# Norm sums in the accumulators of the second layer, and weights loaded in half tiles

## The chip, the core and the metric

The kernel is one program on one core of a Trainium2 chip. The metric is the device time of one execution in microseconds (us), the median of several runs. One further execution was recorded by the hardware profiler; durations of single instructions come from it.

The engines are named as in the profile: PE is TensorE, which multiplies matrices and writes to PSUM; DVE is VectorE, ACT is ScalarE, POOL is GpSimd, and SP is SyncE, which issues all DMAs of this kernel. Each engine works through its own queue strictly in order: an instruction that waits holds up all that stand behind it.

## What is computed

The reference is a trunk of two layers over a sequence of 1024 tokens with 1024 channels, in float32. A layer is a mixer and a feed-forward net (FFN), each wrapped in a norm ahead of it and a norm behind it, whose result is added to the residual:

```
for l in range(2):
    y = rms_norm(h, norm_g[l, 0])
    y = even_mixer(y, ...) if l == 0 else odd_mixer(y, ...)   # y @ w_in, two head groups, cat @ w_out
    h = h + rms_norm(y, norm_g[l, 1])
    y = swiglu(rms_norm(h, norm_g[l, 2]), w_gate[l], w_up[l], w_down[l])
    h = h + rms_norm(y, norm_g[l, 3])
```

`rms_norm(x, g)` is `x * rsqrt(mean(x*x) + 1e-6) * g`, the mean over the 1024 channels of one token. The even mixer has a gated DeltaNet group and a sparse attention group that an indexer selects keys for; the odd mixer has a stick-breaking attention group and a gated linear recurrence (HGRN2).

## The kernel before

**Tiles.** Everything is held feature-major: a tile is 128 channels by 512 tokens, so the residual of one half of the sequence (512 tokens) is 8 tiles. The two halves go through the layers one behind the other and overlap. A weight unit is 128x1024 numbers (512 KB). `wload` (L228) brings it in as one tile `wraw` and splits each number into a high part `whi` (ACT, L193) and a rest `wlo` (DVE for the first 512 columns, POOL for the others, L197). Activations are split in the same way (`yhi`, `ylo`, or two `act` tiles). `passes` (L240) then multiplies high with high, high with rest and rest with high into one bank of PSUM; a unit that makes one tile of 128x512 takes 24 matmuls of 128x512.

**Banks.** PSUM has 8 banks of 128x512. `banks` (L137) shares them out by name, and the kernel does it once: three accumulators (`acc`), one bank `a` for the recurrences, one bank `b`, three banks `w` for the attention. A name with several banks hands them out in turn: the fourth `acc` gets the bank of the first, and its first matmul waits until that one has been read.

**Norms.** The sum over the 1024 channels is a matmul with a tile of ones. The squares of the 8 tiles are made on ACT and added up on DVE into the tile `ssq` (`sumsq`, L290). `inv_rms` (L302) multiplies `ssq` with the ones into a bank, and ACT makes the reciprocal root of it (tile `rs` or `rd`). In the residual and in `norms` (L346) that bank is `b`, which the first stage also uses for DeltaNet chunks.

**Residual.** `residual` (L376) stands behind each output projection and each FFN. It takes a first sum (over the sublayer's output, L380), scales the 8 tiles on DVE (L388), adds the 8 tiles of the residual, which come by DMA into 3 buffers `hld` (L387, L389), and takes a second sum over the result, for the next norm. In the form with `late=True` (behind an FFN of the first layer) all of it is one piece: scaling, adding, the next activation tiles (`y_tile`, L332 on ACT and L336 on DVE), the squares and the second sum (`norms`, L351), and the same sum as a column (L317).

**Order.** A scheduler decides the order on each engine: it simulates the program and takes, among the instructions that are ready in its simulation, those with the highest priority. Code under `first()` has a raised priority. The order is fixed when the kernel is built. The code that matters for the second stage is in `run` (L1279): after `m0.close()` (L1316) the recurrence and stick-breaking attention of the second layer follow, mixed with the rest of the first layer for the second half: `outproj(0, 1)`, `after_out(0, 1)`, `proj_c(0)`, four `stick`s, `ffn(0)`, `after_ffn(0, 1)` with `late=True`, `outproj(1, 0)`, and so on. Output projections (`outproj`, L410) work on two accumulators at a time; the second half of an FFN is eight accumulations, of 12 matmuls each in groups of four units.

**The start.** `first_norm(0)` (L360) loads the first half of x in 8 tiles, makes activation tiles without waiting for the norm, and takes the sums alongside. `proj_even_a` (L566) then computes the unit `U_KI` and twelve units `U_QKV` from them.

Of the kernel before, what the change touches and what calls it, by code (L numbers as in the profile page):

```python
# [13 lines left out]
F32R = mybir.dt.float32r  # L14
# [8 lines left out]
P = 128  # L23
# [4 lines left out]
KD = 8  # L28
# [83 lines left out]
class Trunk:  # L112
# [37 lines left out]
    def consts(self):  # L150
# [6 lines left out]
        with self.first():  # L157
            nc.sync.dma_start(self.gg, self.ins["p_cols"])
            nc.sync.dma_start(self.cc, self.ins["c_main"])
        self.k = self.t(self.np_, [P, 8], "kk")  # L160
# [67 lines left out]
    def wload(self, u):  # L228
        nc = self.nc
        with self.first():  # L230
            raw = self.t(self.wp, [P, 1024], "wraw")
            nc.sync.dma_start(raw, self.ins["w_units"][u])
            w = []
            for c, e in ((slice(0, 512), nc.vector), (slice(512, 1024), nc.gpsimd)):
                w.append(self.split(raw[:, c], *(self.t(self.wp, [P, 512], n, F32R, bufs=4) for n in ("whi", "wlo")), (e,)))
        self.pace()

        return lambda o, n=P: [t[:, o % 512:o % 512 + n] for t in w[o // 512]]

    def passes(self, sums, w, first=True, last=True):  # L240

        mm = self.nc.tensor.matmul
        order = [((0, 0), (0, 1)), ((1, 0),)] if w == 0 else [((0, 0), (1, 0)), ((0, 1),)]
        n = len(sums[0][2]) // 2
        seq = [(g, ps, l[a], r[b]) for pairs in order for part in (slice(0, n), slice(n, None))
               for a, b in pairs for g, ps, terms in sums for l, r in terms[part]]
        begun, end = set(), {g: i for i, (g, *_) in enumerate(seq)}
        for i, (g, ps, l, r) in enumerate(seq):  # L250
            mm(ps, l, r, start=first and g not in begun, stop=last and end[g] == i)  # L251
            begun.add(g)
# [11 lines left out]
    def dense_fm(self, u, y):  # L264
        w = self.wload(u)
        ps = self.acc()
        self.passes([(0, ps, [(w(k * P), y.t[k]) for k in range(KD)])], 0)
        return ps

    def dense_tm(self, u0, y):  # L270
# [75 lines left out]
    def norms(self, y, tiles, rows):  # L346

        acc = None
        for k in range(KD):
            acc = self.sumsq(acc, k, tiles[k])  # L350
        y.r = self.inv_rms(acc, "rd", "b")  # L351
        if rows:
            y.rows = self.inv_rms_rows(acc, "b")

# [5 lines left out]
    def first_norm(self, half):  # L360
        with self.first():
            tiles, acc, y = [], None, Y()
            for k in range(KD):
# [4 lines left out]
                else:  # L368
                    acc = self.sumsq(acc, k, x)
                tiles.append(x)  # L370
            if half:
                return self.to_y(0, 0, tiles, self.inv_rms(acc))
# [3 lines left out]
    def residual(self, l, i, src, dst, parts, acc, nxt, box, late=False):  # L376

        nc = self.nc
        with self.first():
            r = self.inv_rms(acc, "rs", "b")  # L380
            acc = None
# [16 lines left out]
        if nxt is not None and not late:  # L398
            yield
            with self.first():  # L400
                r = self.inv_rms(acc, "rs", "b")
            yield
# [101 lines left out]
    def last_residual(self, src, dst, parts, halves):  # L504
        nc = self.nc
        with self.first():
# [4 lines left out]
            for i, (c, acc) in enumerate(halves):  # L511
                r = self.inv_rms(acc, ("rs", "rd")[i], "b")
                for k in range(KD):
# [52 lines left out]
    def proj_even_a(self, half, y):  # L566
        nc = self.nc
        if half == 0:
# [3 lines left out]
            self.an = self.head_gain(self.cp, "a_norm")  # L572
        ps = self.dense_fm(U_KI, y)
        with self.first():
# [11 lines left out]
        for ct in range(12):  # L586
            ps = self.dense_fm(U_QKV + ct, y)
            with self.first():
# [690 lines left out]
    def run(self):  # L1279
        tc = self.tc  # L1280
        every = lambda gen: deque(gen, maxlen=0)
        self.dn = self.head_gain(self.cp, "d_norm")
        self.banks(acc=3, a=1, b=1, w=3)
        m0 = ExitStack()
        pool = m0.enter_context(tc.tile_pool(name="m0", bufs=1))
# [29 lines left out]
        self.finish()  # L1315
        m0.close()  # L1316
        m1 = ExitStack()
        pool = m1.enter_context(tc.tile_pool(name="m1", bufs=1))
# [145 lines left out]
```

## Time and profile before

| What | us |
|---|---|
| median of 3 runs | 2910.11 (2907.5 to 2910.74) |
| the profiled execution, its own time | 2903.69 |
| its span, first to last instruction | 2901.9 |
| PE busy | 2818.6 (97%) |
| DVE busy | 1694.5 (58%) |
| ACT busy | 1574.0 (54%) |
| POOL busy | 1123.3 (39%) |

The span is what the trace covers; 1.8 us of the execution's own time lie around it. The profiled execution was 6.4 us (0.2%) shorter than the median of the runs. Busy time of PE is a sum over matmuls that overlap each other in a pipeline, so what tells of a loss is time in which PE is not busy, and the clock that it was granted.

### The profile page before, as it was taken

The page shows a single profiled execution, that of the slowest core. Times are in us where ns is not written, and L with a number is a line of the kernel's source. Part 1 is how long each engine was busy: PE and PEld are TensorE (multiplying, and loading weights), DVE is VectorE, ACT ScalarE, POOL GpSimd, SP SyncE. Part 2 cuts the span into 40 slices and gives each one's busy share as a digit, 9 for nine tenths or more (in the row PEclk, how much of TensorE's full clock was granted, in tenths as well). Part 3 has the DMA queues.
Part 4 walks back from the last instruction along what each step waited for, and adds up shares of the span by engine and source line. Part 5 has one row for each costly group of instructions (what it writes and reads, how often), then busy time and mean ns, then how long its engine had stood idle before and what let it go on. Part 6 is the DMA issues. An engine that isn't in the chain of part 4 may idle for free. (4 is left out here: it accounts for less than half of the span.)

```text
span 2901.9 us, 41648 instructions
## 1 busy us (share of the span) xinstructions
PE 2818.6 (97%) x14850; PEld 2351.2 (81%) x14850; DVE 1694.5 (58%) x3037; ACT 1574.0 (54%) x2893; POOL 1123.3 (39%) x916
## 2 busy tenths in 40 slices
PE   8999999999999998999999999999999999999997
PEld 6888888878787886978788888889778778788886
DVE  7857973675656557378665235736666544732235
ACT  5545863666657585254664335536666544543333
POOL 3323332344435342255554332325555432333332
PEclk9999999999999999999999999999999999999999
DMA  5433446243333334446333334654323323543233
GB/s 196 136 121 109 144 151 209 91 146 114 103 117 107 104 121 137 139 147 202 111 109 95 100 97 125 231 156 128 98 87 107 98 89 115 167 149 98 95 95 109
DMA packets 200975, 366.63 MB, mean 126 GB/s; under 512 B 16544, under 2 KB 104640, under 8 KB 200768
## 3 DMA queue, kind: packets, MB, share of 16 engines
q1 hardware_dynamic: 200768, 363.97, 39.6%
q8 instruction: 117, 1.92, 0.3%
q14 instruction: 90, 0.74, 0.1%
HBM read 306.23 MB, written 57.67 MB: 125 GB/s over the span
## 5 line engine op out<-in xcount | busy, mean ns | idle before, releaser
L197 POOL TENSOR_TENSOR wlo<-wraw,whi 128x512 fp32r<-128x512 f32 x422 | 589.1, 1396 | 1240.3 <-PE acc L251 497.3
L193 ACT ACTIVATE whi<-wraw 128x512 fp32r<-128x512 f32 x844 | 521.6, 625 | 487.0 <-PE acc L251 431.2
L197 DVE TENSOR_TENSOR wlo<-wraw,whi 128x512 fp32r<-128x512 f32 x422 | 337.9, 801 | 470.7 <-PE acc L251 355.5
L251 PE MATMUL acc<-yhi,whi 128*128 128x512 f32 x2064 | 585.3, 400 | 11.8 <-ACT whi L193 8.0
L251 PE MATMUL acc<-ylo,whi 128*128 128x512 f32 x2064 | 581.9, 398 | 2.2 <-DVE ylo L336 2.2
L251 PE MATMUL acc<-yhi,wlo 128*128 128x512 f32 x2064 | 536.1, 396 | 0.0
L251 PE MATMUL acc<-act,whi 128*128 128x512 f32 (+1 forms) x1984 | 510.6, 393 | 21.3 <-DVE stage L452 5.7
L251 PEld LDWEIGHTS acc<-yhi,whi 128*128 128x128 f32 x2064 | 386.1, 189 | 99.5 <-ACT whi L193 8.0
L251 PEld LDWEIGHTS acc<-ylo,whi 128*128 128x128 f32 x2064 | 386.3, 189 | 88.3 <-issue 6.0
L251 PEld LDWEIGHTS acc<-yhi,wlo 128*128 128x128 f32 x2064 | 383.7, 188 | 84.1 <-issue 6.1
L251 PEld LDWEIGHTS acc<-act,whi 128*128 128x128 f32 x1984 | 363.1, 189 | 109.3 <-issue 11.5
L251 PE MATMUL acc<-act,wlo 128*128 128x512 f32 (+1 forms) x992 | 266.6, 386 | 1.4 <-POOL wlo L197 1.4
L251 PEld LDWEIGHTS acc<-act,wlo 128*128 128x128 f32 x992 | 182.0, 188 | 38.5 <-POOL wlo L197 1.8
L950 ACT ACTIVATE pen<-sc,tk 128x384 bf16<-128x384 f32 (+4 forms) x155 | 155.3, 1002 | 52.2 <-DVE tk L954 46.1
L480 DVE TENSOR_TENSOR part<-acc,part 128x512 f32<-128x512 f32 x152 | 103.8, 685 | 66.2 <-PE acc L251 66.0
L193 ACT ACTIVATE act<-stage 128x512 fp32r<-128x512 f32 x104 | 65.2, 629 | 136.9 <-DVE stage L459 117.0
L197 POOL TENSOR_TENSOR act<-stage,act 128x512 fp32r<-128x512 f32 x88 | 120.2, 1366 | 43.1 <-ACT act L193 41.0
L299 DVE TENSOR_TENSOR ssq<-ssq,sq 128x512 f32<-128x512 f32 (+1 forms) x119 | 98.7, 830 | 27.2 <-ACT sq L298 25.0
L951 DVE TENSOR_SCALAR tk<-tk 128x1 uint32<-128x1 f32 x186 | 39.3, 211 | 125.4 <-ACT pen L950 124.9
L452 DVE TENSOR_TENSOR stage<-acc,stage 128x512 f32<-128x512 f32 x66 | 45.5, 689 | 98.3 <-ACT stage L220 98.2
L251 PE MATMUL acc<-whi,yhi 128*128 128x256 f32 x640 | 100.1, 287 | 1.6 <-DVE stage L552 1.6
L251 PE MATMUL acc<-whi,ylo 128*128 128x256 f32 x640 | 101.3, 287 | 0.0
(461 smaller groups left out, 4038.1 us busy)
## 6 DMA issues: line engine op xcount, KB each, us to landing
wraw<-in_w_units_dram SPq DMA_DIRECT2D x422, 512.0 KB, 3.6
h<-part SPq DMA_DIRECT2D x40, 256.0 KB, 3.9
hld<-h SPq DMA_DIRECT2D x40, 256.0 KB, 4.6
qkvT<-stage SPq DMA_DIRECT2D x24, 256.0 KB, 2.5
kT<-kbT SPq DMA_DIRECT2D x24, 256.0 KB, 3.6
vv<-vb SPq DMA_DIRECT2D x24, 256.0 KB, 3.0
qkv<-qkvT SPq DMA_DIRECT2D x18, 256.0 KB, 3.6
part<-in_x_dram SPq DMA_DIRECT2D x16, 256.0 KB, 6.3
```

The costliest lines, as they stand in the source:

```text
L193: nc.scalar.activation(hi, src, AF.Copy)
L197: e.tensor_tensor(out=lo[:, c], in0=src[:, c], in1=hi[:, c].bitcast(F32), op=OP.subtract)
L251: mm(ps, l, r, start=first and g not in begun, stop=last and end[g] == i)
L299: nc.vector.tensor_tensor(out=acc, in0=acc, in1=sq, op=OP.add)
L452: nc.vector.tensor_tensor(out=s, in0=pg, in1=s, op=OP.mult)
L480: nc.vector.tensor_tensor(out=parts[d], in0=ps, in1=parts[d], op=OP.add)
L950: sc.activation(pen, s, AF.Sign, scale=sg, bias=nb, accum_out=n)
L951: v.tensor_scalar(rej.bitcast(U32), n, th, float(1 << b), op0=OP.is_lt, op1=OP.mult)
```

## The change

Five edits. (1) After the first stage the banks are shared out anew: four `acc`, one `a`, three `w` and no `b`; a new field `nb` names the bank of the norms' sums, `b` in the first stage and `acc` in the second. (2) A weight unit comes in two half tiles of 128x512 (256 KB), four buffers in place of two of double the size. (3) The first two units, `U_KI` and the first `U_QKV`, are loaded together and multiplied side by side, one channel tile after the other (`dense_pair`). (4) The DMA of the constants `c_main` is issued behind the tiles of x. (5) In `passes` the last third of a product (high times rest of the weight) is no longer cut in two halves when several sums are open.

```diff
@@ consts
             nc.sync.dma_start(self.gg, self.ins["p_cols"])
-            nc.sync.dma_start(self.cc, self.ins["c_main"])
@@ wload
-            raw = self.t(self.wp, [P, 1024], "wraw")
-            nc.sync.dma_start(raw, self.ins["w_units"][u])
             w = []
             for c, e in ((slice(0, 512), nc.vector), (slice(512, 1024), nc.gpsimd)):
-                w.append(self.split(raw[:, c], *(self.t(self.wp, [P, 512], n, F32R, bufs=4) for n in ("whi", "wlo")), (e,)))
+                raw = self.t(self.wp, [P, 512], "wraw", bufs=4)
+                nc.sync.dma_start(raw, self.ins["w_units"][u][:, c])
+                w.append(self.split(raw, *(self.t(self.wp, [P, 512], n, F32R, bufs=4) for n in ("whi", "wlo")), (e,)))
@@ passes
-    def passes(self, sums, w, first=True, last=True):
+    def passes(self, sums, w, first=True, last=True, steps=2):
...
-        n = len(sums[0][2]) // 2
-        seq = [(g, ps, l[a], r[b]) for pairs in order for part in (slice(0, n), slice(n, None))
-               for a, b in pairs for g, ps, terms in sums for l, r in terms[part]]
+        n = len(sums[0][2]) // steps
+        parts = [slice(i * n, (i + 1) * n) for i in range(steps)]
+        high, low = order
+        seq = [(g, ps, l[a], r[b]) for part in parts for a, b in high for g, ps, terms in sums for l, r in terms[part]]
+        seq += [(g, ps, l[a], r[b]) for a, b in low for g, ps, terms in sums for l, r in terms]
@@ new
+    def dense_pair(self, us, y):
+        ws, pss = [self.wload(u) for u in us], [self.acc() for _ in us]
+        self.passes([(i, ps, [(w(k * P), y.t[k]) for k in range(KD)]) for i, (w, ps) in enumerate(zip(ws, pss))], 0, steps=KD)
+        return pss
@@ norms, residual, last_residual
-        y.r = self.inv_rms(acc, "rd", "b")
+        y.r = self.inv_rms(acc, "rd", self.nb)
...
-            r = self.inv_rms(acc, "rs", "b")
+            r = self.inv_rms(acc, "rs", self.nb)
@@ first_norm
+            if half == 0:
+                self.nc.sync.dma_start(self.cc, self.ins["c_main"])
@@ proj_even_a
-        ps = self.dense_fm(U_KI, y)
+        ps, first = self.dense_pair((U_KI, U_QKV), y) if half == 0 else (self.dense_fm(U_KI, y), None)
...
-            ps = self.dense_fm(U_QKV + ct, y)
+            ps = first if half + ct == 0 else self.dense_fm(U_QKV + ct, y)
@@ run
         self.banks(acc=3, a=1, b=1, w=3)
+        self.nb = "b"
...
         m0.close()
+        self.banks(acc=4, a=1, w=3)
+        self.nb = "acc"
```

**PE's queue between the FFN of the first layer (second half) and the output projection behind it.** The names: `acc_...<-act_...,whi_...` or `wlo_...` is a matmul of the FFN or of the projection, `b_...<-ssq_...` or `acc_...<-ssq_...` a norm's sum, `acc_...<-cc_76,ssq_...` the same sum as a column. Before, the FFN's last accumulator is `acc_17005`, and 34 matmuls of the projection (accumulators `acc_17183` and up) stand between it and the first sum, `b_17022`. The second sum, `b_17122`, comes 123 rows behind the first, in the middle of the projection's last accumulator:

```order
L251 MATMUL acc_17422<-act_17149,wlo_17431 128x512
L251 MATMUL acc_17422<-act_17155,wlo_17431 128x512
L306 MATMUL b_17122<-ssq_17099,cc_76 128x512
L251 MATMUL acc_17422<-act_17161,whi_17460 128x512
L251 MATMUL acc_17422<-act_17167,whi_17460 128x512
```

In the changed kernel the FFN's last accumulator is `acc_17493` and the projection's first two are `acc_17671` and `acc_17672`:

```order
L252 MATMUL acc_17493<-act_17239,wlo_17473 128x512
L252 MATMUL acc_17493<-act_17323,wlo_17473 128x512
L313 MATMUL acc_17510<-ssq_17353,cc_76 128x512
L313 MATMUL acc_17610<-ssq_17587,cc_76 128x512
L324 MATMUL acc_17615<-cc_76,ssq_17587 128x1 x4
L252 MATMUL acc_17671<-act_17625,whi_17675 128x512
L252 MATMUL acc_17671<-act_17631,whi_17675 128x512
L252 MATMUL acc_17672<-act_17625,whi_17675 128x512
```

Both sums and the column moved ahead of the whole projection, directly behind the FFN. Everywhere in the second stage the accumulators now start on PE in the order in which the code hands them out, the sums among them.

**DVE's queue at the same place in the changed kernel**, the end of the stretch between the two sums (`part` are the 8 output tiles). From the first sum's last addition on, DVE's queue holds two `act` tiles (L196), eight rows of the form L397 (the scaling), eight L398, eight L343 and seven L306, and no row of another kind, until the second sum's last addition:

```order
L398 TENSOR_TENSOR part_15245<-part_15245,hld_17578 128x512
L306 TENSOR_TENSOR ssq_17587<-ssq_17587,sq_17601 128x512
L343 SCALAR_TENSOR_TENSOR ylo_3787_17575<-part_15230,gg_77,yhi_3786_17574 128x512
L306 TENSOR_TENSOR ssq_17587<-ssq_17587,sq_17604 128x512
L343 SCALAR_TENSOR_TENSOR ylo_3790_17584<-part_15245,gg_77,yhi_3789_17583 128x512
L306 TENSOR_TENSOR ssq_17587<-ssq_17587,sq_17607 128x512
L196 TENSOR_TENSOR wlo_17759<-wraw_17756,whi_17758 128x512
```

The work of the projection on DVE (the activation tiles and the weights of its first two units) moved ahead of these rows, its later weights, from `wlo_17759` on, behind them.

**PE's queue at the end of an output projection**, here that of the second layer's first half. Before, the projection's last accumulator is followed by 32 matmuls of the next projection (`acc_17580`, `acc_17618`), and the sum stands among these:

```order
L251 MATMUL acc_17618<-ylo_3532_17051,whi_17610 128x512
L251 MATMUL acc_17618<-ylo_3535_17060,whi_17610 128x512
L306 MATMUL b_17502<-ssq_17255,cc_76 128x512
L251 MATMUL acc_17618<-yhi_3537_17068,whi_17614 128x512
L251 MATMUL acc_17618<-yhi_3540_17077,whi_17614 128x512
```

Now the sum follows the last accumulator (`acc_17923`) at once, and the next projection (`acc_18086`) stands behind it:

```order
L252 MATMUL acc_17923<-act_17661,wlo_17969 128x512
L252 MATMUL acc_17923<-act_17667,wlo_17969 128x512
L313 MATMUL acc_18006<-ssq_17747,cc_76 128x512
L252 MATMUL acc_18086<-yhi_3768_17520,whi_18076 128x512
L252 MATMUL acc_18086<-yhi_3771_17529,whi_18076 128x512
```

The first sums of the other two output projections of the second stage and the sum behind the FFN of the second layer's first half have moved in the same way.

## Rows read from the trace of the kernel before

**Rows 1.** The page: span, and PE's busy time, share, instructions.

```profile
span 2901.9 us, 41648 instructions
PE 2818.6 (97%) x14850; PEld 2351.2 (81%) x14850; DVE 1694.5 (58%) x3037; ACT 1574.0 (54%) x2893; POOL 1123.3 (39%) x916
```

**Rows 2.** Stretches: length, busy time of five engines, PE's clock, DMA share, GB/s.

```profile
1100.00:1150.00 50.00, 39.14 (x206) 30.89 (x207) 39.34 (x78) 27.09 (x49) 9.55 (x8) 0.86 0.43 142
...
1400.00:1450.00 50.00, 47.84 (x269) 38.83 (x268) 37.29 (x50) 32.19 (x65) 34.94 (x34) 0.97 0.35 115
...
2150.00:2200.00 50.00, 47.88 (x262) 36.36 (x262) 38.74 (x52) 29.02 (x55) 31.93 (x29) 1.00 0.32 99
```

**Rows 3.** PE's waits from 1236 us on: total us, times, longest.

```profile
PE acc L251 <- DVE stage L452: 5.7, 2, 3.5
PE acc L251 <- POOL act L197: 4.8, 6, 2.1
PE b L306 <- DVE ssq L299: 4.4, 3, 2.9
```

**Rows 4.** PE's timeline: the two sums behind the first layer's second FFN.

```profile
1799.39 1.02 PE L306 MATMUL b<-ssq,cc 128*128 128x512 f32 x2
...
1829.02 1.12 PE L306 MATMUL b<-ssq,cc 128*128 128x512 f32 x2 [0.91 <-DVE ssq L299]
```

**Rows 5.** DVE's timeline between these two sums.

```profile
1801.84 6.43 DVE L388 SCALAR_TENSOR_TENSOR part<-part,gg,rs 128x512 f32<-128x512 f32 x8 [1.99 <-ACT rs L309]
1808.19 1.89 DVE L389 TENSOR_TENSOR part<-part,hld 128x512 f32<-128x512 f32 x3
...
1810.60 1.48 DVE L336 SCALAR_TENSOR_TENSOR ylo<-part,gg,yhi 128x512 fp32r<-128x512 f32 x2
...
1828.28 1.28 DVE L299 TENSOR_TENSOR ssq<-ssq,sq 128x512 f32<-128x512 f32 x2
```

**Rows 6.** Timeline: first matmul behind a projection and an FFN, last addition of each.

```profile
2445.80 1.07 PE L251 MATMUL acc<-yhi,whi 128*128 128x512 f32 x4
...
2447.18 1.55 DVE L299 TENSOR_TENSOR ssq<-ssq,sq 128x512 f32<-128x512 f32 x2 [1.34 <-ACT sq L298]
...
2520.24 1.07 PE L251 MATMUL acc<-yhi,whi 128*128 128x512 f32 x4
...
2522.09 0.69 DVE L299 TENSOR_TENSOR ssq<-ssq,sq 128x512 f32<-128x512 f32 x1 [0.76 <-ACT sq L298]
```

**Rows 7.** PE's waits before 1236 us: the longest.

```profile
PE a L744 <- DVE dec L740: 7.0, 1, 7.0
```

**Rows 8.** Timeline of the start, ACT and PE.

```profile
14.17 0.71 ACT L332 ACTIVATE yhi<-part,gg 128x512 fp32r<-128x512 f32 x1
...
15.31 1.13 ACT L193 ACTIVATE whi<-wraw 128x512 fp32r<-128x512 f32 x2
...
24.57 0.42 PE L583 MATMUL acc<-cc,stage 16*128 16x16 f32 x4
...
31.25 0.91 PE L858 MATMUL w<-lg,pt 32*128 32x384 f32 x2
...
33.34 1.09 PE L251 MATMUL acc<-yhi,whi 128*128 128x512 f32 x4
```

**Rows 9.** Timeline of the end, PE and DVE.

```profile
2883.49 1.19 PE L251 MATMUL acc<-act,whi 128*128 128x256 f32 x8 [2.40 <-DVE part L500]
...
2886.01 1.22 PE L251 MATMUL acc<-act,whi 128*128 128x256 f32 x8 [0.85 <-DVE part L500]
...
2892.29 3.25 DVE L515 SCALAR_TENSOR_TENSOR part<-part,gg,rd 128x256 f32<-128x256 f32 x8 [1.75 <-ACT rd L309]
2895.46 2.76 DVE L516 TENSOR_TENSOR part<-part,tail 128x256 f32<-128x256 f32 x8
```

**Rows 10.** DMA issues of the page: KB each, median us to landing.

```profile
wraw<-in_w_units_dram SPq DMA_DIRECT2D x422, 512.0 KB, 3.6
h<-part SPq DMA_DIRECT2D x40, 256.0 KB, 3.9
```

More of the change, by code (lines that the diff above doesn't have):

```diff
@@ L350, in norms @@
             acc = self.sumsq(acc, k, tiles[k])
-        y.r = self.inv_rms(acc, "rd", "b")
+        y.r = self.inv_rms(acc, "rd", self.nb)
         if rows:
-            y.rows = self.inv_rms_rows(acc, "b")
+            y.rows = self.inv_rms_rows(acc, self.nb)
     def part(self):
@@ L400, in residual @@
             with self.first():
-                r = self.inv_rms(acc, "rs", "b")
+                r = self.inv_rms(acc, "rs", self.nb)
             yield
@@ L511, in last_residual @@
             for i, (c, acc) in enumerate(halves):
-                r = self.inv_rms(acc, ("rs", "rd")[i], "b")
+                r = self.inv_rms(acc, ("rs", "rd")[i], self.nb)
                 for k in range(KD):
```

## The prediction

> **What bounds the kernel now.** I read the page first: of a span of 2901.9 us PE is busy 2818.6 us [rows 1], so 83.3 us is all that any rearrangement of waits can win, and every new wait on PE comes nearly whole on top of the time. The stretches come next. In the one from 2150 us on, PE was idle for 2.1 us and kept clock 1.00; in the one from 1400 us on it was idle as long and was granted 0.97; in the one from 1100 us on it was idle for 10.9 us and was granted 0.86 [rows 2]. So a wait of 2 us costs, in about every second case, another 3% of 50 us = 1.5 us, and a long one 14% of 50 us = 7.0 us. Third come PE's waits: from 1236 us on, which is about where the second stage begins, the three largest are 5.7, 4.8 and 4.4 us in total [rows 3]; before that one of 7.0 us stands out [rows 7]. The norms' sums scarcely hold PE up: of 4.4 us, 2.9 belong to the very last one.
>
> **The price of the sums' new place.** The order decides this case. In the kernel before, a sum stands dozens of matmuls behind the last accumulation whose squares it adds up, and PE works in between. In the changed one the sum follows that accumulation at once, and PE, which takes its queue strictly in order, stands still until the last tile is evacuated, squared and added.
>
> How long that takes is in the trace of before. Behind an output projection the next matmul starts at 2445.80 and the last addition ends at 2447.18 + 1.55 = 2448.73: 2.95 us (2.9 rounded is also what the last sum waited, [rows 3]). Behind an FFN: 2520.24 to 2522.09 + 0.69 = 2522.78, 2.55 us [rows 6]. Five sums move so, three behind projections and two behind FFNs: 3 x 2.95 + 2 x 2.55 = **+14.0 us**. The clock: by the two stretches above half of such waits draw 1.5 us after them. These are a little longer than those of 2.1 us, so I take four of the five, **+6.0 us** (bounds 3.0 for two and 7.5 for all).
>
> **The long wait.** Behind the second half's FFN of the first layer, both sums and the column come before any matmul of the output projection. Between the two sums the whole residual has to be done, with PE idle. Its chain on DVE: from the first sum's start to the first scaling 1801.84 - 1799.39 = 2.45 us [rows 4, 5]; eight scalings 6.43; then eight additions, eight activation rests and seven additions of squares. Singly these take 1.89/3 = 0.63, 1.48/2 = 0.74 and 1.28/2 = 0.64 us [rows 5], so 5.0 + 5.9 + 4.5 = 15.4. In all 24.3 us, less the two sums' own time on PE, which was paid before too (0.9): **+23.4 us**. Bounds: if all 31 operations took 0.63, 19.5 + 2.45 = 22.0, so 21.1 net; if the stretch took as long as before, 1829.02 - 1799.39 = 29.6 [rows 4], 28.7 net. In that one DVE also worked on weights, which now stand behind, and at 1812.68 the fourth addition waited for its `hld` tile, so I stay near the lower bound. In the chain nothing covers it: the projection's matmuls, which covered all of it before, are queued behind the second sum, and with them the evacuations, the projection's later weights and everything behind. The clock behind a wait of this length is bounded by 0 and by the 7.0 of the stretch from 1100 us on; I take the middle, **+3 us**: that stretch held more waits than one.
>
> **What drops out.** The earlier waits for sums, 4.4 in total less the 2.9 of the last one: **-1.5 us** [rows 3].
>
> **The fourth accumulator.** The waits for L452 and for POOL's `act` tiles are those of a down product on the last activation tile of its group. PE can go ahead with those matmuls that need only the earlier tiles, five for each accumulator that is free: two pairs of high and rest for two tiles, and one. One more bank is 5 x 0.226 = 1.13 us of cover; 0.226 is the distance between starts in a train of equal matmuls, (2446.71 - 2445.80)/4 [rows 6]. Twice 1.13 off the 5.7 us, and of the 4.8 us in six waits all but 1.0 (the longest is 2.1): 2.3 + 3.8 = **-6 us**, and one clock drop less, **-1.5 us**. Bounds: nothing (where the order takes the bank for a sum instead), and the whole 10.5 us.
>
> **The start.** Now each of the first unit's matmuls waits for its activation tile, and the second unit starts after the sums; the third starts at 33.34 us [rows 8]. Side by side, both units' 32 high products are fed by the same activation tiles, the last of which ends on ACT at 14.17 + 0.71 = 14.9; ACT has two more weight conversions ahead of it, 1.13 us [rows 8], so about 18.5 on PE. Then come 16 matmuls with the rest of the weights, 3.6 us, the sums, the column and the transposes, some 2.8 us: the third unit at about 24.9. That is 8.4 us earlier, of which 2.1 us come back, since two L858 (0.91 each) and a smaller piece move behind: **-6.3 us**. Bounds: -8.4, and -3 if DVE and ACT are late with a second unit's weights. The later `c_main` is needed first by the sums and lands long before.
>
> **The end.** The last sum but one moves to eight matmuls before the end, and the residual of its half, sixteen operations on DVE, behind the last evacuation. The tail grows by about 2.7 us; the two waits of 2.40 and 0.85 us for evacuations, which DVE delayed with that residual, go [rows 9]. Net **-0.5 us**. The residual behind the last sum (3.25 + 2.76 us) stays as it was.
>
> **First stage.** The first stage keeps its banks. Its order changes through the half tiles and the start: the attention's work on DVE stands a dozen rows earlier against DeltaNet's decay around 1100 us. The wait of 7.0 us there [rows 7] may shrink; **-3 us**, bounds -7 and +6 (it grows by what one such row group takes).
>
> **Half tiles.** 422 loads become 844. A 512 KB load lands 3.6 us after its issue, a 256 KB transfer 3.9 [rows 10], so a unit is there no earlier and not much later; PE takes 24 x 0.226 = 5.4 us for a unit, and the DMA engines are busy 32 to 43% in the stretches shown [rows 2]. I cost it at **0**; without that cover it would be a few us at each unit whose load starts late. The Trainium skill ("DMA: Bandwidth & Descriptors", sections "Anatomy of one DMA" and "Bandwidth") speaks against this edit: it gives each transfer about 2.0 us of fixed cost and 436 GB/s, and asks for batches of 1 MiB or more. By its figures a unit would take 5.2 us in two transfers one behind the other instead of 3.2 (my estimate from the page); the trace has no such step between 256 and 512 KB, and either number stays below a unit's matmuls, so the sum is the same.
>
> **Sum.** +14.0 + 6.0 + 23.4 + 3 - 1.5 - 6 - 1.5 - 6.3 - 0.5 - 3 = **+27.6 us**. The profiled execution of 2903.69 us becomes 2931.3. It stood 6.4 us below the median of the runs, so the median goes to 2910.11 + 27.6 = **2937.7 us**.
>
> **Rivals.** *Worse (0.17).* The long wait takes 28.7 instead of 23.4, because the `hld` tiles (three buffers, so five of the eight loads wait for a buffer inside the chain) land late with no other work between; the clock behind it costs the full 7.0, and all five short waits draw the clock: +5.3 + 4.0 + 1.5 = +10.8, 2948.5 us. For it speaks the wait for `hld` at 1812.68 [rows 5]; against it that it was 0.61 us long and the only one.
>
> *Faster (0.06).* The sums cost nothing: four banks turn, the evacuation and the squares of one overlap the next group's matmuls. Then only the gains stay, -1.5 - 6 - 1.5 - 6.3 - 0.5 - 3 = -18.8 us, 2891.3 us. It decides if the six places together hold PE for less than 18.8 us; the changed order speaks against it, since no matmul stands between the last accumulation and its sum for PE to do. The Trainium skill ("Perfetto Trace Analysis", section "Matmuls") would have it so: independent groups should rotate through the banks so that ACT and DVE evacuate one beside the next. By that rule a fourth bank wins; here the bank is free, and it is the queue's order that holds PE, so the trace gives the rule no say.
>
> *No change (0.05).* The first stage's new order gives back what the second loses: it would have to remove more than a quarter of the 83.3 us that PE is idle in all [rows 1], 22 us at least beyond my -3. About 2910 us.
>
> *Late weights (0.02).* Half tiles start late behind other transfers on SP's queue; 0.1 us at each of 422 units is +42 us, 2980 us. Against it: the wait for weights was never among the largest.
>
> **Chances and range.** The forecast holds 0.70, with its own range from 2925 (lower bounds of the long wait, -2.3, of the clocks, -3 and -3, of the first stage, -4) to 2948. At the low end I add another 7 us for gains of the fourth bank and the start at their bounds: 2918. At the high end the worse rival, with no gain from the fourth bank, 2948.5 + 7.5, and the first stage at nothing, +3: 2960. What this kernel's measurement can tell from no change is 0.2%, 5.8 us. Faster 0.06, same 0.05, slower 0.89.
>
> **What would show it.** Right: PE idle once for 20 us or more in front of two sums at about 1800 us, with DVE at work throughout; five waits for `ssq` of 2.5 to 3 us; a half clock behind most of them; the third unit at about 25 us; no waits for weights. Wrong: sums that wait for less than 1 us, a chain between the two sums that does not run on DVE alone, or a loss or gain of over 10 us before 1236 us, where I have the least to go by.

## The result

The changed kernel takes 2936.91 us (median of 4 runs, 2932.68 to 2940.58) against 2908.81 us before: the ratio is 1.0096 with an interval of 1.0078 to 1.0114, or 28 us more. The forecast was 2937.7 us. The sum came out because errors in four of its parts cancelled, one of them a wait that I had not foreseen; the largest term was right. The experiments below take that apart.

The page of the changed kernel answers to [rows 1]: PE's busy time grew by only 7.7 us, the span by 35.9. The profiled execution (2939.68 us) was 2.8 us above the median of its runs, that of before 5.1 below, so the two traces lie 8 us further apart than the medians.

```profile
span 2937.8 us, 42374 instructions
PE 2826.3 (96%) x14850; PEld 2358.8 (80%) x14850; DVE 1668.6 (57%) x3037; ACT 1583.7 (54%) x2893; POOL 1125.6 (38%) x916
```

PE's waits in the changed kernel over the whole span (total us, times, longest). The line of `inv_rms` is now L313, that of `passes` L252. The sums, 4.4 us in [rows 3], are now 40.5; all of these waits lie behind 1236 us too. The wait for L452 (now L461) and most of that for POOL's `act` are gone. The wait of 7.0 us in [rows 7] has shrunk to 4.7. A wait of 8.5 us for L561 is new.

```profile
PE acc L313 <- DVE ssq L306: 40.5, 7, 23.7
PE acc L252 <- DVE stage L561: 9.6, 2, 8.5
PE acc L252 <- ACT whi L192: 5.8, 1, 5.8
PE a L753 <- DVE dec L749: 4.7, 1, 4.7
...
PE acc L252 <- POOL act L196: 1.5, 1, 1.5
```

The place of the long wait in PE's timeline, which answers to [rows 4]. The sums run at 1794.28 and 1820.09 us; nothing runs on PE between them.

```profile
1789.19 1.07 PE L252 MATMUL acc<-act,wlo 128*128 128x512 f32 x4
1794.28 2.08 PE L313 MATMUL acc<-ssq,cc 128*128 128x512 f32 x2 [4.02 <-DVE ssq L306]
1820.09 2.07 PE L313 MATMUL acc<-ssq,cc 128*128 128x512 f32 x2 [23.74 <-DVE ssq L306]
1821.96 1.71 PE L324 MATMUL acc<-cc,ssq 128*128 128x1 f32 x8
```

DVE's timeline there, which answers to [rows 5]. DVE works through the residual nearly without a gap: idle for 0.42 and 1.17 us while `hld` lands.

```profile
1792.02 1.60 DVE L196 TENSOR_TENSOR act<-stage,act 128x512 fp32r<-128x512 f32 x1
1793.54 0.68 DVE L306 TENSOR_TENSOR ssq<-ssq,sq 128x512 f32<-128x512 f32 x1
...
1798.33 5.39 DVE L397 SCALAR_TENSOR_TENSOR part<-part,gg,rs 128x512 f32<-128x512 f32 x8 [0.55 <-ACT rs L316]
1803.63 1.89 DVE L398 TENSOR_TENSOR part<-part,hld 128x512 f32<-128x512 f32 x3
...
1808.01 0.69 DVE L398 TENSOR_TENSOR part<-part,hld 128x512 f32<-128x512 f32 x1 [0.42 <-DMA hld<-h]
...
1811.81 0.69 DVE L398 TENSOR_TENSOR part<-part,hld 128x512 f32<-128x512 f32 x1 [1.17 <-DMA hld<-h]
...
1819.36 0.68 DVE L306 TENSOR_TENSOR ssq<-ssq,sq 128x512 f32<-128x512 f32 x1
```

The other sums on PE, in order: behind the first projection, the second, the third, the FFN of the second layer, and at the end. The first waits 0.28 us only: two groups of the recurrence (L1234, L1242) stand on PE ahead of it and cover it.

```profile
1303.32 1.13 PE L313 MATMUL acc<-ssq,cc 128*128 128x512 f32 x2 [0.28 <-DVE ssq L306]
...
1872.25 1.99 PE L313 MATMUL acc<-ssq,cc 128*128 128x512 f32 x2 [2.86 <-DVE ssq L306]
...
2483.22 1.97 PE L313 MATMUL acc<-ssq,cc 128*128 128x512 f32 x2 [2.86 <-DVE ssq L306]
...
2559.11 1.13 PE L313 MATMUL acc<-ssq,cc 128*128 128x512 f32 x2 [2.44 <-DVE ssq L306]
...
2925.75 1.22 PE L313 MATMUL acc<-ssq,cc 128*128 128x256 f32 x2 [4.35 <-DVE ssq L306]
```

The clock behind the waits, in windows (us, busy time of PE, PEld, DVE, ACT, POOL, then granted clock, DMA share and GB/s). The 10 us behind the long wait were granted 0.70, a loss of 3.0 us, and the next ten 1.00. The 10 us from the second and the third projection's sum on were granted 0.83, 1.7 us each. A sum's two passes took 2.0 us there, 1.1 at the full clock. The sum at 1794.28, behind a wait of 4.02 us, took 2.08 us as well.

```profile
1822.00:1832.00 10.00, 10.00 (x37) 8.36 (x36) 0.69 (x1) 3.05 (x6) 0.55 (x1) 0.70 0.00 0
1832.00:1842.00 10.00, 10.00 (x45) 8.28 (x45) 1.55 (x3) 4.88 (x8) 2.16 (x2) 1.00 0.37 105
...
1872.00:1882.00 10.00, 9.75 (x34) 7.23 (x35) 6.54 (x11) 2.58 (x4) 1.35 (x1) 0.83 0.08 26
...
2483.00:2493.00 10.00, 9.78 (x34) 7.27 (x35) 6.55 (x11) 4.01 (x7) 1.39 (x1) 0.83 0.09 26
```

The start on PE, which answers to [rows 8]: the first matmul comes at 5.76 us (8.04 before), the sixteen low products at 18.77, the third unit at 26.02 (33.34 before).

```profile
5.76 0.80 PE L252 MATMUL acc<-yhi,whi 128*128 128x512 f32 x1 [5.76 <-ACT whi L192]
...
18.77 3.79 PE L252 MATMUL acc<-yhi,wlo 128*128 128x512 f32 x16
...
26.02 2.08 PE L252 MATMUL acc<-yhi,whi 128*128 128x512 f32 x4
```

### The profile page after: what moved, and what is told of

Same layout as the page of the kernel before. It is cut to its first block, busy times and chain, and to the rows that moved or that the text cites. A ratio compares the mean times of both kernels' runs of the same rounds, so it can differ in the third digit from the quotient of the medians.

```text
span 2937.8 us, 42374 instructions
## 1 busy us (share of the span) xinstructions
PE 2826.3 (96%) x14850; PEld 2358.8 (80%) x14850; DVE 1668.6 (57%) x3037; ACT 1583.7 (54%) x2893; POOL 1125.6 (38%) x916
## 5 line engine op out<-in xcount | busy, mean ns | idle before, releaser
L196 POOL TENSOR_TENSOR wlo<-wraw,whi 128x512 fp32r<-128x512 f32 x422 | 588.7, 1395 | 1324.1 <-PE acc L252 614.9
L196 DVE TENSOR_TENSOR wlo<-wraw,whi 128x512 fp32r<-128x512 f32 x422 | 345.5, 819 | 447.8 <-PE acc L252 346.9
L252 PE MATMUL acc<-yhi,whi 128*128 128x512 f32 x2064 | 586.2, 400 | 8.5 <-ACT whi L192 5.8
L252 PE MATMUL acc<-ylo,whi 128*128 128x512 f32 x2064 | 579.8, 397 | 1.7 <-DVE ylo L343 1.3
L252 PE MATMUL acc<-yhi,wlo 128*128 128x512 f32 x2064 | 535.2, 395 | 0.0
L252 PE MATMUL acc<-act,whi 128*128 128x512 f32 (+1 forms) x1984 | 505.1, 392 | 13.6 <-DVE stage L561 8.5
L252 PEld LDWEIGHTS acc<-yhi,whi 128*128 128x128 f32 x2064 | 386.7, 190 | 95.8 <-issue 8.1
L252 PEld LDWEIGHTS acc<-ylo,whi 128*128 128x128 f32 x2064 | 387.3, 189 | 88.5 <-DVE ylo L343 5.3
L252 PEld LDWEIGHTS acc<-yhi,wlo 128*128 128x128 f32 x2064 | 383.8, 188 | 84.6 <-issue 6.4
L252 PEld LDWEIGHTS acc<-act,whi 128*128 128x128 f32 x1984 | 367.8, 191 | 95.9 <-ACT sq L219 8.7
L252 PE MATMUL acc<-act,wlo 128*128 128x512 f32 (+1 forms) x992 | 265.2, 386 | 0.0
L252 PEld LDWEIGHTS acc<-act,wlo 128*128 128x128 f32 x992 | 182.3, 188 | 37.0 <-issue 1.7
L196 POOL TENSOR_TENSOR act<-stage,act 128x512 fp32r<-128x512 f32 x88 | 120.0, 1364 | 37.7 <-ACT act L192 34.2
L306 DVE TENSOR_TENSOR ssq<-ssq,sq 128x512 f32<-128x512 f32 (+1 forms) x119 | 101.6, 854 | 16.5 <-ACT sq L305 13.2
L461 DVE TENSOR_TENSOR stage<-acc,stage 128x512 f32<-128x512 f32 x66 | 45.6, 690 | 110.4 <-ACT stage L219 110.2
L252 PE MATMUL acc<-whi,yhi 128*128 128x256 f32 x640 | 97.9, 288 | 1.5 <-DVE stage L561 1.1
L252 PE MATMUL acc<-whi,ylo 128*128 128x256 f32 x640 | 96.0, 285 | 0.0
```

Of the source, the lines that this page charges most:

```text
L196: e.tensor_tensor(out=lo[:, c], in0=src[:, c], in1=hi[:, c].bitcast(F32), op=OP.subtract)
L306: nc.vector.tensor_tensor(out=acc, in0=acc, in1=sq, op=OP.add)
L461: nc.vector.tensor_tensor(out=s, in0=pg, in1=s, op=OP.mult)
```

## The experiments

The theory: the loss is the place of the sums in PE's queue. The first rival: it comes from the half tiles or the new start. The ratios are to runs of the kernel before on the same chip; us are medians. Where a step is counted in us, it is a difference of ratios times 2908 us.

**1. The sums in a bank of their own, all else as changed (own_bank).**

```diff
         m0.close()
-        self.banks(acc=4, a=1, w=3)
-        self.nb = "acc"
```

> The changed kernel without its first edit: three accumulators, and the norms' sums in a bank of their own to the end. Theory (the loss is the sums' place in PE's queue): all six waits for sums go, 14.0 + 23.4 us and the clock behind them 9 us; the start's gain and the first stage's stay, so 2909 - 6 - 3 = 2900 us (2894 to 2906), and PE waits for sums less than 6 us in all before the last one. Rival (half tiles or the new start cost the time): 2930 us or more, as the changed kernel.

Measured: 2890.83 us, ratio 0.9951 (0.9937 to 0.9964), 3 us below the range that I gave. The loss is in the first edit, and the rival falls: half tiles and start together win 14 us, more than the 9.3 that I gave them. The only wait for a sum left in PE's list is the last one:

```profile
PE b L313 <- DVE ssq L306: 4.0, 1, 4.0
```

**2. The first edit alone, on the kernel before (banks_only).**

```diff
         m0.close()
+        self.banks(acc=4, a=1, w=3)
+        self.nb = "acc"
```

> The kernel before with the first edit alone: four accumulators in the second stage, sums in them; whole weight tiles, the old start. Theory: the whole loss and none of the start's gain, 2909 + 14.0 + 6.0 + 23.4 + 3 - 1.5 - 7.5 = 2946 us (2938 to 2954), a wait of 22 to 25 us between two sums. Rival (the loss needs the half tiles): 2909 to 2915 us.

Measured: 2950.52 us, ratio 1.0151 (1.0137 to 1.0165). The edit costs 44 us by itself, 4.5 us above the value that I expected and inside its range; the longest wait for a sum is 22.3 us. It does not need the half tiles.

**3. Only the sums behind the first layer's second FFN elsewhere (late_w).**

```diff
         r = self.after_ffn(0, 1, f, y, True)
+        self.nb = "w"
         next(r)
+        self.nb = "acc"
```

> The changed kernel, with the two sums and the column behind the first layer's second FFN in a bank of the attention (w) in place of the accumulators; the other sums as changed. Theory: the wait of 24.4 us between the sums and that of 4.2 us ahead of them go, and the clock behind them, 3 us: 2937 - 31 = 2906 us (2902 to 2911); the four other first sums still hold PE for 2.5 to 3 us each. Rival (PE would have waited there anyway, for DVE's residual, at the next activation tiles): 2925 us or more.

Measured: 2906.48 us, ratio 0.9996 (0.9987 to 1.0005). This one place is worth 1.00%, 29 us; PE would not have waited there for the residual otherwise. In PE's order the second of the two sums stands 130 matmuls behind the first, in the kernel before 123, and the projection's matmuls are between them again. Five waits for sums remain, the last included:

```profile
PE acc L313 <- DVE ssq L306: 12.9, 5, 4.4
PE acc L252 <- DVE stage L561: 9.1, 2, 8.5
```

**4. The banks opened anew, with the shares that they had (repool).**

```diff
         m0.close()
-        self.banks(acc=4, a=1, w=3)
-        self.nb = "acc"
+        self.banks(acc=3, a=1, b=1, w=3)
```

> As own_bank, but the banks are closed and opened again between the stages with the same shares as before. In the changed kernel PE waits 8.5 us at 1239 us for the last evacuation of the first stage, which I had not foreseen. Theory (opening the banks anew makes the first accumulators of the second stage wait for the old ones): the wait comes back here and not in own_bank, 3 to 8 us above own_bank. Rival (that wait comes from the order that the first edits made, or from the fourth accumulator's place): the same as own_bank within 2 us.

Measured: 2899.80 us, ratio 0.9975 (0.9965 to 0.9985), 7 us above own_bank by the ratios and 9 by the medians. Opening the banks anew costs that by itself. The traces place it: repool is level with own_bank at its 6600th matmul, at 1232 us, 9.4 us behind at its 8000th, at 1486 us, and 10.5 at its last. Its first matmul of the second stage waits for the last evacuation of the first (L561):

```profile
1249.32 2.90 PE L252 MATMUL acc<-act,whi 128*128 128x512 f32 x6 [8.53 <-DVE stage L561]
```

In own_bank PE passes the same place at 1240.59 us without a wait, and waits only once it comes to the accumulator whose bank is not yet read:

```profile
1238.67 2.08 PE L252 MATMUL acc<-wlo,yhi 128*128 128x256 f32 x16
1240.59 2.00 PE L252 MATMUL acc<-act,whi 128*128 128x512 f32 x8
...
1246.03 2.11 PE L252 MATMUL acc<-act,whi 128*128 128x512 f32 x8 [1.03 <-DVE stage L561]
```

**5. Opened anew, but the accumulators in banks that have been idle (reopen_w).** Experiment 4 gave the accumulators the numbers 1 to 3, the same banks in which the first stage's last units lie. Handing out `w` first moves them to 4 to 6.

```diff
         self.banks(acc=3, a=1, b=1, w=3)
+        for _ in range(3):
+            self.mx("w")
```

> As the run with the same shares opened anew (2899.8 us), but the second stage's attention banks (w) are handed out first, so that the accumulators lie in the attention's old banks, which have long been idle, and not in the old accumulators' banks. PE's order is the same but for a few rows. Theory (the first accumulators of the second stage get banks that the last units of the first stage still hold): the 8.5 us at 1240 us shrink to below 2 and the time to 2891 us (2888 to 2895). Rival (opening banks anew waits for all old ones): 2899 us or more.

Measured: 2899.77 us, ratio 0.9964 (0.9950 to 0.9978). My theory fell: the wait is as long as before, although no matmul has written to the accumulator's bank since about 1159 us.

```profile
1235.55 2.08 PE L252 MATMUL acc<-wlo,yhi 128*128 128x256 f32 x16
1246.15 4.23 PE L252 MATMUL acc<-act,whi 128*128 128x512 f32 x10 [8.52 <-DVE stage L561]
```

So the rival holds: what is opened anew waits for the old share as a whole, not for the bank that it takes. It is the program that says so, not the chip. In the order with its waits, this first matmul waits for DVE and ACT in own_bank, and for PE as well in reopen_w. What tells is the count that it awaits of DVE: 1683 operations in own_bank, 1703 in reopen_w and repool, and the 1703rd is the evacuation (L561) of the first stage's last accumulator.

```
L252 MATMUL acc_2874_13271<-act_2851_13225,whi_2877_13275 128x512 [waits DVE_49,Activation_49]
L252 MATMUL acc_2878_13278<-act_2855_13232,whi_2881_13282 128x512 [waits DVE_49,PE_49,Activation_49]
```

**6. Four accumulators, all sums in the attention's banks (sums_w).**

```diff
         self.banks(acc=4, a=1, w=3)
-        self.nb = "acc"
+        self.nb = "w"
```

> The changed kernel with four accumulators and the banks opened anew, but all the norms' sums of the second stage in the attention's banks (w): no sum holds PE. Against the run with three accumulators and the same reopening (2899.8 us) only the fourth accumulator differs. Theory (the prediction's term): 7.5 us less, 2892 us (2889 to 2897); against the run with the late sums alone in w (2906.5 us) three waits of 2.86, 2.86 and 2.44 us and two clock drops go, some 12 us. Rival (the fourth accumulator is worth nothing, since other waits end last): 2899 to 2902 us.

Measured: 2898.55 us, ratio 0.9962 (0.9947 to 0.9976), above the 2889 to 2897 of my theory. Against repool (0.9975) that is 0.13%, 4 us, and the two intervals overlap: by the times, the fourth accumulator's gain can be told neither from zero nor from the 9 us that I had given it. The two kernels differ in the sums' bank too, and the last sum waits longer in the attention's bank. Its wait in repool, then in sums_w:

```profile
PE b L313 <- DVE ssq L306: 4.0, 1, 4.0
```

```profile
PE w L313 <- DVE ssq L306: 6.8, 1, 6.8
```

In the traces sums_w is 3.8 us ahead of repool at the 14700th of 14850 matmuls and 2.1 at the end of the span. Against late_w it is 0.34%, 10 us: the price of the four other places. I had expected that no sum would hold PE; the last one does.

**7. The half tiles alone (half_only) and the start alone (start_only),** each on the kernel before: edit 2 of the change, and edits 3 to 5.

> The kernel before with the half tiles alone. Theory (prediction's cost of nothing, but in the trace the first weights are ready 2.3 us earlier): 2908 - 2 = 2906 us (2903 to 2909). Rival 1 (transfers of 256 KB cost): 2912 us or more. Rival 2 (smaller buffers that come free earlier take out waits for weights all along and carry most of the 17 us that the changed kernel without its banks gained): 2900 us or less.

> The kernel before with the start alone (two units side by side, constants behind x, the last third of a product uncut), whole weight tiles. Theory (the prediction's term): 2908 - 6.3 = 2902 us (2899 to 2905). Rival (start and half tiles only work together, since side by side the first units need four conversions of weights early): 2905 us or more. If it comes to 2896 us or less, the start's order carries gains into the first stage that I sized too small.

Measured: half_only 2884.52 us, ratio 0.9913 (0.9900 to 0.9927), the best of all kernels here; start_only 2895.85 us, ratio 0.9952 (0.9939 to 0.9964). Half tiles win 25 us where I wrote 0, the start 14 where I wrote 6.3; both times lie below the range of my theory. half_only came at the number of its second rival, start_only at that of the last case, gains carried into the first stage; its trace agrees, 3.3 us ahead at the 1000th matmul and 9.6 at the 6000th, at 1138 us. Together (own_bank) they win 14, not 39: they don't add up. In half_only the largest waits for activation tiles in the second stage, L452 with 5.7 us and POOL's `act` with 4.8 [rows 3], are gone or small, with three accumulators and no other edit:

```profile
PE b L306 <- DVE ssq L299: 5.0, 3, 4.0
...
PE acc L251 <- POOL act L197: 1.5, 4, 0.4
```

These are the waits that I had given to the fourth accumulator. They were gone before it came.

**8. One tile, two transfers (two_dma).**

```diff
             raw = self.t(self.wp, [P, 1024], "wraw")
-            nc.sync.dma_start(raw, self.ins["w_units"][u])
             w = []
             for c, e in ((slice(0, 512), nc.vector), (slice(512, 1024), nc.gpsimd)):
+                nc.sync.dma_start(raw[:, c], self.ins["w_units"][u][:, c])
```

> The kernel before with a weight unit still in one tile of 512 KB and two buffers, but loaded by two transfers of 256 KB. It tells apart why the half tiles alone gave 25 us (2884.5). Theory 1 (the first half lands earlier, so its conversion starts earlier; buffers play no part): 2885 to 2892 us. Theory 2 (a half tile's buffer comes free as soon as its own conversion is done, so the next load starts earlier): no gain without separate tiles, 2904 to 2912 us. In between, each has a share.

Measured: 2890.19 us, ratio 0.9932 (0.9918 to 0.9947): four fifths of the gain without separate tiles, as theory 1 expected. But how long ACT waits for weights does not go with the time. These rows are ACT's waits for `wraw` (total us, times, longest), in the order before, two_dma and half_only:

```profile
ACT whi L193 <- DMA wraw<-in_w_units_dram: 37.0, 21, 3.6
```

```profile
ACT whi L193 <- DMA wraw<-in_w_units_dram: 34.1, 29, 3.4
```

```profile
ACT whi L193 <- DMA wraw<-in_w_units_dram: 13.7, 12, 2.3
```

So with separate tiles ACT waits 20 us less, and the time is 5 us less, a difference at which the two intervals still overlap. The median load landed 2.9 us after its issue in two_dma, 2.7 in half_only, 3.6 before [rows 10].

**9. Only the constants behind x (cmain_only).**

```diff
             nc.sync.dma_start(self.gg, self.ins["p_cols"])
-            nc.sync.dma_start(self.cc, self.ins["c_main"])
```

and the same line in `first_norm`, behind the eight loads of x.

> The kernel before with the constants' load behind the tiles of x and nothing else. PE's order changes in some 70 places, nearly all at the start. Theory (the start's gain is the units side by side, and the constants only stand in the way of x by one transfer): 1 to 3 us less, 2906 to 2908 us. Rival (small shifts in the scheduler's order alone are worth as much as the 13.5 us of the start): 2902 us or less, or 2914 or more.

Measured: 2904.02 us, ratio 0.9979 (0.9969 to 0.9988), 6 us. That is between the two: one transfer moved is worth 3 to 9 us. In its trace PE is 1.6 us ahead at its first matmul, 3.7 us at its 1500th, at about 285 us, and 3.3 at its last. By subtraction 8 us of the start's 14 are left for the units side by side and the uncut last third; no run has these without the transfer.

**10. One sharing for both stages with four accumulators and two banks for the attention (acc4_w2).**

```diff
-        self.banks(acc=3, a=1, b=1, w=3)
+        self.banks(acc=4, a=1, b=1, w=2)
```

> The changed kernel with one sharing of the banks for both stages: four accumulators, one a, one b for the sums, and two w in place of three; nothing is opened anew. Theory: against the run with three accumulators and three w (2890.8 us) the fourth accumulator wins up to 7.5 us and the third w's absence costs the attention waits, above all at the pairs of L927 and L1044 that wait 2 to 4 us already: 2885 to 2900 us; if the accumulators are what counts below 2890.8, if the attention's banks are, above.

Measured: 2976.05 us, ratio 1.0221 (1.0206 to 1.0237), far outside. At its 12000th matmul, at about 2250 us, it is 20 us ahead of own_bank, 15 of them won by the 6600th, at 1217 us; behind that the second half's stick-breaking attention runs by itself with two banks, and PE waits for ACT at each step, with the clock at 0.62:

```profile
PE w L1085 <- ACT cah L1082: 42.1, 13, 4.6
...
2350.00:2500.00 150.00, 81.26 (x181) 40.97 (x180) 39.94 (x61) 49.19 (x87) 20.66 (x20) 0.62 0.12 37
```

The 20 us ahead suggest that a fourth accumulator in both stages, without opening anything, is worth something after all. No run here separates that from the attention's share.

**11. The candidate (half_acc4):** half tiles, four accumulators in idle banks, sums in the attention's banks, the old start.

> The candidate from the experiments: the kernel before with half tiles, no change to the start, four accumulators in the second stage that lie in banks idle at that point, and the sums in the attention's banks. If reopening costs nothing there and the fourth accumulator is worth nothing measurable (2898.6 against 2899.8 us), 2884 us (2880 to 2889), as the half tiles alone; if the fourth accumulator wins its 7.5 us after all, 2878 us; if reopening still costs, 2892.

Measured: 2897.35 us, ratio 0.9951 (0.9937 to 0.9966), 11 us above half_only by the ratios and 13 by the medians, and 5 above the worst of my three numbers. It waits 8.2 us for the last evacuation, as reopen_w does, and its last sum waits 6.6 us against 4.0. In the traces it falls 13.5 us behind half_only between 1230 and 1482 us; what the reopening costs beyond its wait is open. The version to keep is half_only.

## Why the prediction came out, point by point

Five kernels lead step by step from the kernel before to the changed one. Each step is the difference of two ratios times 2908 us; each ratio has an interval of 3 to 5 us either way, a difference of two one of about 5 to 6.

| Step | read from | predicted | measured |
|---|---|---|---|
| half tiles, start, first stage | own_bank | 0 - 6.3 - 3 = -9.3 | -14 |
| opening the banks anew | repool | not named | +7 |
| fourth accumulator, earlier waits for sums | sums_w | -6 - 1.5 - 1.5 = -9.0 | -4 |
| the four other first sums, their clock, the end | late_w | 11.5 + 4.8 - 0.5 = +15.8 | +10 |
| the long wait, the sum ahead of it, clock | changed kernel | 2.55 + 23.4 + 3 + 1.2 = +30.1 | +29 |
| sum | | +27.6 | +28 |

**The sum hit by luck.** The five rows miss by -4.7, +7, +5, -5.8 and -1 us. Four of them miss by 5 to 7 us, about as much as the intervals of the rows, and the errors add up to less than 1.

**The long wait was right in place, chain and size.** PE was idle 23.74 us between the sums where I had 23.4, DVE worked nearly throughout on the 31 operations that the order showed, and the clock cost 3.0 us, and 1.0 more in the second sum itself. The parts differ: from the first sum's start to the first scaling it took 4.05 us instead of 2.45, the eight scalings took 5.39 instead of 6.43, and `hld` cost 0.42 + 1.17 us that I had not put in. The sum ahead of it waited 4.02, not 2.55: DVE's queue held an `act` tile of 1.60 us between the last evacuation and its square's addition.

**The other first sums were mis-sized.** Two of them waited 2.86 and 2.86 us for 2.95, that behind the FFN 2.44 for 2.55: right. "Five sums move so" was wrong for the first projection: the recurrence's matmuls in the order ahead of its sum cover it, 0.28 us. So of the five waits that I put at 2.5 to 3 us three came about so, and one was below 1 us, which I had named as a sign of being wrong. The clock fell behind three of the five, the 4.02 us one and the two of 2.86, not behind four. The last sum, where I saw a small gain, waits 4.35 us; but it waits 4.0 in own_bank and half_only too, where its bank is its own, so the first edit is not the cause.

**The start came as worked out, but a little late, and what it won did not last:** the third unit came at 26.02 us, not 24.9, and the wait in front of DeltaNet's decay shrank by 2.3 us, not 3. (The sixteen low products came at 18.77, close to the 18.5 of the prediction, which gives no row for the 2.5 us between ACT's end at 16.0 and there.) Counted by matmuls, the changed kernel is 4.5 us ahead at the 100th, 2.4 at the 1000th and 4.4 at the 6000th, at 1143 us, where I had 9.3 in all; own_bank is 3.0 ahead there and wins 9 of its 14 us behind the 12000th, at about 2250 us. The trace of before is 5 us faster than its median, so some of that may be missing.

**The fourth accumulator was priced twice over.** I costed each edit against the waits of the kernel before, and two edits claimed the same waits: in half_only those for L452 and POOL's `act` are gone or small with three accumulators, in banks_only they are gone with whole tiles. Its measured row, -4 us with an interval of 5 either way, leaves room for zero and for the -9.0.

**Half tiles at 0 was wrong.** I compared the landing of a 512 KB load, 3.6 us, with that of another tile's 256 KB transfer, a store of the residual, 3.9 [rows 10], and concluded that a unit is there no earlier. A weight's own halves landed in a median of 2.7 us, and ACT can start on the first. The Trainium skill's rule in "DMA: Bandwidth & Descriptors" ("Bandwidth") asks for large transfers; here twice as many transfers took 0.87% less time. My estimate from its figures, 5.2 us for a unit's two transfers one behind the other, does not describe loads that overlap; and the Trainium skill gives these figures for transfers that GpSimd issues, where here SP issues all. What the 25 us consist of is not settled: two_dma shows that most of it does not need separate tiles, but PE's order differs in many rows between any two of these kernels, and their gains do not add.

**Opening the banks anew was missed.** I read the change of shares as a relabelling, and read the order for rows that moved, not for the waits of its rows; these would have shown it.

**The rival on the other side** (faster, the sums covered, 2891.3 us) comes close to the time of own_bank, 2890.83 us, the change without its sums on PE's path. The agreement is chance: the rival's sum counts 7.5 us for a fourth accumulator, which own_bank doesn't have. The kernel that has it and keeps the sums out of the way is sums_w, 2898.55 us. The rival's condition, that a group's evacuation overlaps the next group's matmuls, is the rule of "Perfetto Trace Analysis" ("Matmuls") in the Trainium skill; late_w and sums_w agree with it as soon as the next group is allowed ahead of the sum: the long wait is gone in both.

## What to carry to other kernels

A small reduction that shares its buffers with the main accumulators is bound to their order, and an engine that works strictly in order then stands still for the whole chain that feeds it; give it a buffer that the next group doesn't need, even a busy one. Cost the edits of one change one behind the other, each against what the last has left, since two of them may claim one wait. Where a change closes and opens a set of buffers, look at what the first instruction behind it waits for. And where a forecast of many terms comes out, check the terms one by one before you trust it.

## What the runs showed of the hardware

The clock came back fast. Around the long wait it cost 1.0 us in the first sum (behind the wait of 4.02 us), 1.0 in the second (behind that of 23.74), 3.0 in the 10 us behind, and nothing in the next ten; each wait of 2.86 us cost 1.7 us, the sum included, and the one of 2.44 us nothing (2556 to 2580 us, below). So nearly ten times the idle time, 27.8 us, cost about three times as much.

```profile
2556.00:2580.00 24.00, 21.56 (x93) 17.19 (x93) 15.90 (x24) 10.25 (x17) 7.44 (x5) 1.00 0.52 170
```

A second thing was DVE: eight scalings of the same form took 5.39 us where POOL was idle (busy 0.00 of the 25 us below) and 6.43 in [rows 5]. The traces say more. Of the eight in [rows 5], seven took 0.74 us each and one 1.78; that one started within the only POOL operation that ran beside them, at 1805.35 us. Two POOL operations beside the eight, at 1305.87 us in the changed kernel, made it 7.18 us. But it can also go the other way: at 1875.66 us the eight took 5.39 us, and the POOL operation that started among them, a weight's rest as at 1805.35 us, took 3.97. That the two engines hold each other up fits all of these; no run tried it by itself.

```profile
1795.00:1820.00 25.00, 1.35 (x2) 0.00 (x0) 20.71 (x32) 11.51 (x19) 0.00 (x0) 0.50 0.56 185
```

POOL beside the eight scalings: its operation in the kernel before, then DVE and POOL at two places of the changed kernel:

```profile
1805.35 1.71 POOL L197 TENSOR_TENSOR wlo<-wraw,whi 128x512 fp32r<-128x512 f32 x1 [4.34 <-PE acc L251]
```

```profile
1305.87 7.18 DVE L397 SCALAR_TENSOR_TENSOR part<-part,gg,rs 128x512 f32<-128x512 f32 x8 [1.27 <-ACT rs L316]
...
1875.66 5.39 DVE L397 SCALAR_TENSOR_TENSOR part<-part,gg,rs 128x512 f32<-128x512 f32 x8 [3.46 <-ACT rs L316]
```

```profile
1305.79 1.04 POOL L843 TENSOR_TENSOR zt<-zt,orso 128x512 f32<-128x512 f32 x1
...
1310.07 1.77 POOL L196 TENSOR_TENSOR wlo<-wraw,whi 128x512 fp32r<-128x512 f32 x1 [3.24 <-PE acc L252]
...
1880.65 3.97 POOL L196 TENSOR_TENSOR wlo<-wraw,whi 128x512 fp32r<-128x512 f32 x1 [9.79 <-PE acc L252]
```
